# A 512-column product ahead of the 240-column one, at the double pairs that follow a block output part

## The chip, the cores and the metric

The kernel runs on one core of a Trainium2 chip. The metric is the device time of one execution in microseconds, as the median of repeated executions of the same program. The profile shows one of them, engine by engine: PE (TensorE, its weight loads listed apart as PEld), DVE (VectorE), ACT (ScalarE), POOL (GpSimd) and SP (SyncE, which issues most loads).

## The reference

One decoder block on 512 tokens of width 1024, in float32: a feed-forward network, a token mixer, a second feed-forward network, each behind a norm and with a gated residual. The change lies in the two networks. Each multiplies 1024 to 2 x 2816 columns, combines the halves, and multiplies 2816 back to 1024:

```
def swiglu(u, w_in, w_out):
    a, b = jnp.split(u @ w_in, 2, axis=-1)
    return (jax.nn.silu(a) * b) @ w_out
...
    u = modulate(rmsnorm(h, g_norm_ffn1[l]), sh1, sc1)
    h = h + 0.5 * gt1 * swiglu(u, w_ffn1_in[l], w_ffn1_out[l])
    u = modulate(rmsnorm(h, g_norm_mix[l]), sh2, sc2)
    h = h + gt2 * token_mixing(u, cos, sin, w_in[l], w_pool[l], pool_scale[l],
                               w_pool_branch[l], w_attn_branch[l], w_out[l])
    u = modulate(rmsnorm(h, g_norm_ffn2[l]), sh3, sc3)
    h = h + 0.5 * gt3 * swiglu(u, w_ffn2_in[l], w_ffn2_out[l])
return rmsnorm(h, g_final)
```

## The kernel before

Everything is kept transposed: features on the 128 partitions, the 512 tokens along the row. A float32 operand is split into a high and a low part (whi and wlo for weights, UH and UL for the network's input, HI and HK for the hidden values), and each product of the algorithm is three matmuls on PE: high x high, high x low, low x high. Weights come by DMA into the buffers raw and X, ACT writes the high part into the ring whi, and DVE (or ACT and a summing DMA of POOL) writes the low part into wlo.

The 22 hidden tiles of 128 columns, each with an a and a b half, are the "pairs" of a network. `PARTS` cuts them into five parts: 0 to 3, 4 to 7, 8 to 11, 12 to 15, 16 to 21. After each part its hidden tiles are multiplied with the rows of the output matrix and added to the residual H, so that only one part's hidden values are kept. The first pairs of a network are plain: 512-column matmuls. From the 7th pair on in the first network, from the 5th in the second, two pairs are made together by `duo`, a "double pair": token halves of 256 columns and feature halves form 2 x 2 blocks, and seven block products stand in for eight, at the price of sums of blocks on DVE and POOL. Each block product (`product`) is 24 matmuls of 256 columns. The output parts of parts 1, 2 and 3 (`BLOCKED`) are made the same way by `out_block`: seven block products of 24 matmuls, the first begun inside the last double pair of that part. Its later products wait for hidden values that DVE has just split into HI and HK. The output parts of parts 0 and 4 are plain again: 512-column matmuls, with 256-column ones at the very end.

So PE sees, per network, a run of 512-column products (part 0), then 256-column ones to the end of part 4's double pairs, then 512 again. Parts 2 and 3 are two double pairs and a block output part, 3 x 168 = 504 matmuls of 256 columns; part 4 is three double pairs, 504 too.

Two things in the code take account of where such runs meet. `room` shifts the weights in the ring by `SHIFT` = 16 columns for all chunks that are used with 256-column products. And `settle` issues one matmul of 240 columns whose result is overwritten: it writes into the bank that the next real product starts anew. `product` does this when its argument `extra` is set, which `ffn` does for the first double pair of each part.

Within a network, instructions are first recorded and then put in order: `Recorder.flush` walks a plan with a cost for each instruction, keeps PE's order as written, and picks on DVE, ACT, POOL and SP at each moment the instruction that is latest. The code's own order on PE therefore stands, and the other engines' order follows from the plan. All that is recorded has line 318 in the profile.

Of the kernel before, what the change touches and what calls it, by code (L numbers as in the profile page):

```python
# [136 lines left out]
BLOCKED = (1, 2, 3)  # L137
# [7 lines left out]
def pairs_before(n, part):  # L145

    k1 = PARTS[part][1]
    return k1 + 2 if n == 0 and part == 0 else k1
# [17 lines left out]
class Recorder:  # L166
# [24 lines left out]
    def add(self, eng, method, a, k):  # L191
        aps = lambda xs: [x for x in xs if hasattr(x, "tensor") and hasattr(x, "ap")]
        outs = aps(a[:1]) + aps([k.get("accum_out")])
        ins = aps(a[1:]) + aps(v for n, v in k.items() if n != "accum_out")
        i, deps = len(self.ops), set()
        ru = [u for x in ins for u in self.units(x)]
        wu = [u for x in outs for u in self.units(x)]
        for u in ru:
            if u in self.written:
                deps.add(self.written[u])  # L200
        for u in wu:
            if u in self.written:
                deps.add(self.written[u])
            deps.update(self.read.get(u, ()))
        for u in ru:
            self.read.setdefault(u, set()).add(i)
        for u in wu:
            self.written[u] = i
            self.read[u] = set()
        f = None  # L210
        if eng == "ACT" and method == "activation":
            f = self.SETS.get(a[2], a[2])
        elif method == "preload_act_table":
            f = a[0]
        if f is not None:
            now, at, users = self.table
            if f != now:
                deps.update(users)
                if at is not None:
                    deps.add(at)  # L220
                self.table = [f, i, []]
            else:
                deps.add(at)
                users.append(i)
        deps.discard(i)
        self.ops.append((eng, method, a, k, deps, outs, ins))
        return None
# [94 lines left out]
class Kernel:  # L322
# [6 lines left out]
    def plan(self):  # L329
# [52 lines left out]
        def ffn(n, ins, outs, first):  # L382
# [4 lines left out]
            for part, (k0, k1) in enumerate(PARTS):  # L387
# [11 lines left out]
                if part not in BLOCKED:  # L399
                    if n and part + 1 < len(PARTS):  # L400
                        self.added.update(range(len(self.order), len(self.order) + KT // 2))
                    plain(recs)

        ffn(0, f1i, f1o, FIRST)
        shift(4)
        base = len(self.order)
# [5 lines left out]
        self.shifted.update(range(base, base + 4))  # L412
        shift(3)
        ffn(2, f2i, f2o, 0)
        shift(5)
        self.fetched = self.done = self.made = 0
# [584 lines left out]
    def product(self, bank, u, start, extra=0, before=lambda: None):  # L1001
        M = self.nc.tensor.matmul
        before()
        w = self.take()
        if extra:
            self.settle(bank, w[0][0], self.UH[0])
        for p in range(2):
            o = bank[:, p * HT:(p + 1) * HT]
            for k in range(4):
                (hi, lo), (uh, ul) = w[4 * p + k], u[k]  # L1010
                M(o, hi, uh, start=start and p == 0 and k == 0, stop=False, skip_group_check=True)  # L1011
                M(o, hi, ul, start=False, stop=False, skip_group_check=True)  # L1012
                M(o, lo, uh, start=False, stop=k == 3, skip_group_check=True)  # L1013
# [202 lines left out]
    def ffn(self, n, j, last=None):  # L1216
# [10 lines left out]
            self.begin()  # L1227
        for part, (k0, k1) in enumerate(PARTS):
            tail = part + 1 == len(PARTS)
            extra = 1  # L1230
            while j < pairs_before(n, part):
                if j < PLAIN[n]:
                    self.ffn_pair(j, beside)
                    j += 1
                else:
                    own = part in BLOCKED and j + 2 == k1
                    if own and n == 0:
                        last = self.beside_out(part) or last
                    self.duo(n, j, last, tail and j + 2 == FT, extra, self.todo if own else None)
                    last, extra = None, 0  # L1240
                    j += 2
            if part in BLOCKED:
                continue
            if n == 0:
                if part == 0:
                    self.end()
                    last = self.beside_out(part)
                    self.begin()
                else:
                    last = self.beside_out(part) or last  # L1250
            if tail and n:
                self.end()
            nc, v = self.nc, self.nc.vector
            nk = k1 - k0
            hk = [self.plain_of(k) for k in range(k0, k1)]
            if not tail:
                for m in range(0, KT, 2):
                    self.look(4)
                    w = self.take()
                    bs = [self.nb(), self.nb()]  # L1260

                    for ka, kb in ((0, nk - 1), (nk - 1, nk)) if m == 0 else ():
                        for i in range(2):
                            for k in range(ka, kb):
                                self.mm3(bs[i], *w[nk * i + k], *hk[k], k == 0, k == nk - 1)
                    for i, b in enumerate(bs):
                        for k in range(nk if m else 0):
                            self.mm3(b, *w[nk * i + k], *hk[k], k == 0, k == nk - 1)
                        v.scalar_tensor_tensor(self.H[m + i], b, gate[:, m + i:m + i + 1], self.H[m + i],
                                               op0=OP.mult, op1=OP.add)  # L1270

                        if self.todo:
                            self.todo.pop(0)()
                    self.step()
                continue

            def ks(m):
                w = self.take()
                self.split_hi()
                return [(hi, lo, *hk[k]) for k, (hi, lo) in enumerate(w)]  # L1280

            self.look()
            if n == 2:
                self.sums.close()
                op = self.f2.enter_context(self.tc.tile_pool(name="f2o", bufs=1))
                self.OO = op.tile([P, KT * T], F32, name="out").rearrange("p (m t) -> p m t", m=KT)
                self.O = [self.OO[:, m, :] for m in range(KT)]

            kl = [ks(0), ks(1)]
            bs = [self.nb(), self.nb()]  # L1290
            for ka, kb in ((0, nk - 2), (nk - 2, nk)):
                for m in range(2):
                    for k in range(ka, kb):
                        self.mm3(bs[m], *kl[m][k], k == 0, k == nk - 1)
            for m in range(3 if n else 4):
                if m > 1:
                    bs.append(self.nb())
                    for k, x in enumerate(ks(m)):
                        self.mm3(bs[m], *x, k == 0, k == nk - 1)
                v.scalar_tensor_tensor(self.H[m], bs[m], gate[:, m:m + 1], self.H[m], op0=OP.mult, op1=OP.add)  # L1300
                add = self.sumsq(m, self.H[m])
                if n == 2:
                    nc.scalar.activation(self.O[m], self.H[m], AF.Copy, scale=self.g(3)[:, m:m + 1])
                self.split_lo()
                add()
                if m:
                    self.split(self.done)
                self.fetch()
            if n:
                self.out_end((3, 4, 5, 6, 7), ks, gate)  # L1310
            else:
                self.out_tail((4, 5, 6, 7), ks, gate, 1, lambda m: self.X[0][:, m % 2 * HT:])
                self.end()
# [851 lines left out]
```

## Time and profile before

| | |
|---|---|
| median of 3 runs | 1001.5 us (999.51 to 1003.51) |
| the profiled execution's own time | 999.64 us |
| its span, first to last instruction | 997.9 us |
| mean granted TensorE clock | 0.997 |
| PE busy | 980.0 us, 7120 matmuls |
| DVE busy | 798.1 us |
| ACT busy | 550.9 us |
| first 240-column product behind 512-column ones in a double pair | 102.90 us, second network 716.83 us |
| 240-column products at parts 2, 3, 4, first network | 149.46, 209.86, 269.40 us |
| 240-column products at parts 2, 3, 4, second network | 776.22, 836.69, 894.90 us |

Times in the profile count from the first instruction. A matmul is listed from its start to its modelled end, some 0.28 us for 256 columns, and the next begins long before that end; the pace of PE is therefore the distance between starts, or the count of matmuls in a stretch, and not the listed duration. A stretch's count includes those that began shortly before it.

### The profile page before, as it was taken

How to read it: one execution, taken by the hardware profiler on the slowest of the kernel's cores; microseconds unless marked ns; L12 is line 12 of the kernel's file. 1: busy time of each engine (PE TensorE's matmuls, PEld its weight loads, DVE VectorE, ACT ScalarE, POOL GpSimd, SP SyncE). 2: the span in 40 equal slices, each digit the busy share in tenths (PEclk: the TensorE clock that was granted, in tenths of full speed). 3: DMA queues.
4: the chain of work that ended last, by engine and by line, in shares of the span. 5: the costliest groups of instructions: out<-in, count | busy, mean ns of one | idle time of the engine just before them, and what ended most of it. 6: DMA issues, size and time to landing. Idle time of an engine off the chain costs nothing.

```text
span 997.9 us, 17750 instructions
## 1 busy us (share of the span) xinstructions
PE 980.0 (98%) x7120; PEld 911.8 (91%) x7120; DVE 798.1 (80%) x1194; ACT 550.9 (55%) x827; POOL 96.3 (10%) x108
## 2 busy tenths in 40 slices
PE   9999899999999999999999999999999999999997
PEld 7888889999999899778879998998899999999997
DVE  7989899898998866898887766894677868888654
ACT  5454466747665544445645553475367575676553
POOL 0000111111100000005301000001011010110002
PEclk9999999999999999999999999999999999999999
DMA  9856997988988615665236536537568576785602
GB/s 348 275 196 223 268 246 185 237 240 213 241 211 232 195 39 164 227 202 168 63 127 168 148 97 208 183 89 198 157 170 190 148 190 179 194 202 151 183 1 86
DMA packets 55974, 180.65 MB, mean 181 GB/s; under 512 B 7505, under 2 KB 10705, under 8 KB 55890
## 3 DMA queue, kind: packets, MB, share of 16 engines
q1 hardware_dynamic: 44224, 140.18, 42.5%
q0 software_dynamic: 11088, 38.80, 20.7%
q8 instruction: 56, 0.92, 0.4%
q10 hardware_dynamic: 578, 0.53, 0.2%
q14 instruction: 28, 0.23, 0.1%
HBM read 135.29 MB, written 2.24 MB: 138 GB/s over the span
## 4 chain that ended last, share of the span: by engine, by line
PE 86%; DVE 6%; issue 2%; DMA 2%; ACT 2%; SPq 1%; POOL 0%; POOLq 0%; DVEq 0%; ACTq 0%
PE bank L318 52%; PE bank L566 6%; PE bank L568 6%; PE bank L567 6%; PE bank L1011 2%; PE bank L1012 2%; PE bank L1013 2%; PE bank L2091 2%; PE bank L2093 1%; PE bank L2095 1%; DVE wlo L318 1%; DVE hf L318 1%; PE bank L1766 1%; PE bank L1468 1%; DMA X<-wf1i 1%
## 5 line engine op out<-in xcount | busy, mean ns | idle before, releaser
L318 PE MATMUL bank<-UH,whi 128*128 128x256 f32 (+2 forms) x680 | 195.8, 290 | 0.0
L318 PE MATMUL bank<-UL,whi 128*128 128x256 f32 (+1 forms) x672 | 194.9, 290 | 0.1
L318 PE MATMUL bank<-UH,wlo 128*128 128x256 f32 (+1 forms) x672 | 194.7, 290 | 0.0
L318 ACT ACTIVATE whi<-X 128x1024 fp32r<-128x1024 f32 (+3 forms) x121 | 117.1, 982 | 53.5 <-DVE X L318 26.7
L318 PE MATMUL bank<-HK,whi 128*128 128x256 f32 (+1 forms) x472 | 142.4, 302 | 3.5 <-DVE HK L318 2.2
L318 DVE TENSOR_TENSOR wlo<-X,whi 128x1024 fp32r<-128x1024 f32 (+3 forms) x111 | 124.3, 1132 | 23.5 <-ACT whi L318 23.3
L318 PE MATMUL bank<-HI,wlo 128*128 128x256 f32 (+1 forms) x472 | 141.0, 299 | 1.3 <-DVE H L318 1.2
L318 PE MATMUL bank<-HI,whi 128*128 128x256 f32 (+2 forms) x473 | 141.1, 299 | 0.0
L318 PEld LDWEIGHTS bank<-UH,whi 128*128 128x128 f32 x680 | 128.8, 190 | 2.6
L318 PEld LDWEIGHTS bank<-UL,whi 128*128 128x128 f32 x672 | 126.2, 188 | 2.8 <-DVE UL L702 0.3
L318 PEld LDWEIGHTS bank<-UH,wlo 128*128 128x128 f32 x672 | 126.2, 188 | 2.5
L318 PE MATMUL bank<-SH,whi 128*128 128x256 f32 x408 | 114.9, 282 | 3.4 <-ACT bank L318 3.4
L318 PE MATMUL bank<-SL,whi 128*128 128x256 f32 x408 | 114.6, 281 | 0.0
L318 PE MATMUL bank<-SH,wlo 128*128 128x256 f32 x408 | 114.6, 281 | 0.0
L318 PEld LDWEIGHTS bank<-HK,whi 128*128 128x128 f32 x472 | 88.8, 188 | 9.5 <-DVE HK L318 4.4
L318 ACT ACTIVATE whi<-raw 128x1024 fp32r<-128x1024 f32 (+3 forms) x94 | 80.8, 880 | 28.1 <-PE bank L318 15.4
L318 PEld LDWEIGHTS bank<-HI,wlo 128*128 128x128 f32 x472 | 88.6, 188 | 5.3 <-DVE H L318 1.4
L318 PEld LDWEIGHTS bank<-HI,whi 128*128 128x128 f32 x473 | 89.0, 188 | 3.6
L536 DVE TENSOR_TENSOR wlo<-raw,whi 128x1024 fp32r<-128x1024 f32 (+5 forms) x68 | 74.9, 1114 | 16.8 <-ACT whi L519 16.8
L318 DVE TENSOR_TENSOR wlo<-raw,whi 128x1024 fp32r<-128x1024 f32 (+3 forms) x79 | 77.0, 994 | 8.0 <-ACT whi L318 8.0
L318 PEld LDWEIGHTS bank<-SH,whi 128*128 128x128 f32 x408 | 78.5, 192 | 3.5 <-ACT bank L318 3.5
L318 PEld LDWEIGHTS bank<-SL,whi 128*128 128x128 f32 x408 | 77.3, 189 | 0.0
(388 smaller groups left out, 2256.2 us busy)
## 6 DMA issues: line engine op xcount, KB each, us to landing
raw<-wmix SPq DMA_DIRECT2D x44, 512.0 KB, 3.9
raw<-wf1i SPq DMA_DIRECT2D x31, 512.0 KB, 5.5
raw<-wf2i SPq DMA_DIRECT2D x29, 512.0 KB, 4.4
ada<-wada SPq DMA_DIRECT2D x23, 512.0 KB, 5.4
X<-X POOLq DMA_DIRECT2D x23, 512.0 KB, 4.8
AR<-wada SPq DMA_DIRECT2D x19, 512.0 KB, 5.0
raw<-raw POOLq DMA_DIRECT2D x16, 512.0 KB, 5.5
X<-wf2i SPq DMA_DIRECT2D x15, 512.0 KB, 4.6
```

The lines of the kernel that those rows point to most:

```text
L318: getattr(self.real[eng], method)(*a, **k)
L536: self.nc.vector.tensor_tensor(self.lo[:, y], r[:, x], self.hi[:, y], op=OP.subtract)
L566: M(ps, hi, uh, start=start, stop=False)
L567: M(ps, hi, ul, start=False, stop=False)
L568: M(ps, lo, uh, start=False, stop=stop)
L1011: M(o, hi, uh, start=start and p == 0 and k == 0, stop=False, skip_group_check=True)
L1012: M(o, hi, ul, start=False, stop=False, skip_group_check=True)
L1013: M(o, lo, uh, start=False, stop=k == 3, skip_group_check=True)
L1468: nc.tensor.matmul(S[:, o], q[:, toks], k[:, ks], start=True, stop=True, skip_group_check=True)
L1766: M(b, uh, hi, start=k == 0, stop=False)
L2091: M(b, hi, self.UH[k], start=k == 0, stop=False)
L2093: M(b, hi, self.UL[k], start=False, stop=False)
```

## The change

`ffn` now sets `extra` to 2 instead of 1 for the first double pair of a part whose predecessor has a block output part: parts 2, 3 and 4 of both networks, six places. `product` then issues one more matmul ahead of the 240-column one, with the same weights and the same bank, over all 512 columns of UH. Its result is overwritten as well.

```
@@ product
         w = self.take()
+        if extra > 1:
+            M(bank, w[0][0], self.UH[0], start=True, stop=True, skip_group_check=True)
         if extra:
             self.settle(bank, w[0][0], self.UH[0])
@@ ffn
-            extra = 1
+            extra = 1 + int(part - 1 in BLOCKED)
```

On PE, at the start of part 2 of the first network (149.46 us): the last products of the block output part (into bank 95), then the double pair's first block product (bank 93). Before:

```order
L318 MATMUL bank_95<-HK,whi 128x256
L318 MATMUL bank_95<-HI,wlo 128x256
L318 MATMUL bank_93<-UH,whi 128x240
L318 MATMUL bank_93<-UH,whi 128x256
L318 MATMUL bank_93<-UL,whi 128x256
```

and after:

```order
L318 MATMUL bank_95<-HK,whi 128x256
L318 MATMUL bank_95<-HI,wlo 128x256
L318 MATMUL bank_93<-UH,whi 128x512
L318 MATMUL bank_93<-UH,whi 128x240
L318 MATMUL bank_93<-UH,whi 128x256
L318 MATMUL bank_93<-UL,whi 128x256
```

One row is new. Nothing else on PE changes in the whole program but the same row at the five other places.

The plan that orders the other engines counts the longer PE queue, and rows on DVE, ACT, POOL and SP change places from part 2 of the first network on and in the second network. On DVE, at the end of the second double pair of part 2 in the second network (the rows of the trace from 818 us; hf are the hidden values before they are split, X and raw weight buffers). Before:

```order
L318 TENSOR_TENSOR HK<-hf,HI 128x256
L318 TENSOR_TENSOR HK<-hf,HI 128x1024
L318 TENSOR_TENSOR X<-raw_63,raw_65 128x1024
L318 TENSOR_TENSOR wlo<-raw_65,whi 128x512 x2
L318 TENSOR_TENSOR wlo<-raw_64,whi 128x1024
L318 SCALAR_TENSOR_TENSOR H<-bank_95,mod,H 128x256 x2
```

and after:

```order
L318 TENSOR_TENSOR HK<-hf,HI 128x256
L318 TENSOR_TENSOR wlo<-raw_65,whi 128x512
L318 TENSOR_TENSOR HK<-hf,HI 128x1024
L318 TENSOR_TENSOR wlo<-raw_65,whi 128x512
L318 TENSOR_TENSOR wlo<-raw_64,whi 128x1024
L318 SCALAR_TENSOR_TENSOR H<-bank_95,mod,H 128x256
```

A low half of weights has moved ahead of the 1024-wide HK, and the sum of two weight blocks stands earlier, outside the excerpt. The instructions are the same.

More of the change, by code (lines that the diff above doesn't have):

```diff
@@ L1004, in product @@
         w = self.take()
+        if extra > 1:
+            M(bank, w[0][0], self.UH[0], start=True, stop=True, skip_group_check=True)
         if extra:
@@ L1229, in ffn @@
             tail = part + 1 == len(PARTS)
-            extra = 1
+            extra = 1 + int(part - 1 in BLOCKED)
             while j < pairs_before(n, part):
```

## The prediction

> **What bounds the kernel now.** I read the head of the page first, for the bound; then a table of stretches, each cut from one 240-column product to the next; then the order of time on PE around those products; then the waits of PE.
>
> ```profile
> span 997.9 us, 17750 instructions
> PE 980.0 (98%) x7120; PEld 911.8 (91%) x7120; DVE 798.1 (80%) x1194; ACT 550.9 (55%) x827; POOL 96.3 (10%) x108
> PEclk9999999999999999999999999999999999999999
> PE 86%; DVE 6%; issue 2%; DMA 2%; ACT 2%; SPq 1%; POOL 0%; POOLq 0%; DVEq 0%; ACTq 0%
> ```
>
> PE is busy for 98% of the span, the chain that ended last is PE for 86%, and the granted clock stays at nine tenths or more. So time is saved only by issuing less on PE or by issuing the same faster. The second is possible, because equal products do not cost the same everywhere. In the next rows (stretch, its length, then busy time and number of instructions for PE, PEld, DVE, ACT, POOL) the first number behind PE's busy time is the point:
>
> ```profile
> 197.40:209.80 12.40, 12.40 (x112) 12.40 (x111) 11.83 (x19) 7.00 (x10) 0.89 (x1) 1.00 1.01 287
> 210.00:250.00 40.00, 40.00 (x342) 40.00 (x341) 35.55 (x47) 24.96 (x34) 6.06 (x7) 1.00 0.77 206
> 827.00:836.60 9.60, 9.60 (x84) 9.60 (x83) 7.17 (x10) 4.13 (x6) 0.86 (x1) 1.00 0.77 237
> 838.00:876.00 38.00, 38.00 (x337) 38.00 (x337) 32.16 (x41) 24.03 (x33) 4.81 (x6) 1.00 0.74 186
> 718.00:758.00 40.00, 40.00 (x356) 40.00 (x355) 28.25 (x35) 26.45 (x37) 6.06 (x7) 1.00 0.73 176
> 533.00:548.00 15.00, 15.00 (x135) 15.00 (x134) 11.48 (x15) 9.38 (x14) 0.85 (x1) 1.00 0.62 172
> ```
>
> All are 256-column products, PE never idles in them, and the clock is 1.00 in each. A product is listed for 0.28 us while the next begins after about 0.115, so some 2.4 of each count were already under way when the stretch began. Then 40.00 us hold 339.6 products in the second row (117.8 ns each) and 353.6 in the fifth (113.1 ns). There are two paces, which I call tight (about 113.3 ns from start to start) and wide (117.8): first, fourth, fifth and sixth row are tight, second and third wide. What changes the pace is seen in the order of time (start, duration, form; "x2" joins the 240-column product and the 256-column one behind it):
>
> ```profile
> 209.74 0.28 PE L318 MATMUL bank<-HI,wlo 128*128 128x256 f32 x1
> 209.86 0.39 PE L318 MATMUL bank<-UH,whi 128*128 128x240 f32 x2
> 836.57 0.28 PE L318 MATMUL bank<-HI,wlo 128*128 128x256 f32 x1
> 836.69 0.40 PE L318 MATMUL bank<-UH,whi 128*128 128x240 f32 x2
> 716.38 0.39 PE L318 MATMUL bank<-HK,whi 128*128 128x512 f32 x1
> 716.60 0.39 PE L318 MATMUL bank<-HI,wlo 128*128 128x512 f32 x1
> 716.83 0.39 PE L318 MATMUL bank<-UH,whi 128*128 128x240 f32 x2
> 530.20 0.39 PE L568 MATMUL bank<-YH,wlo 128*128 128x512 f32 x1
> 530.42 0.27 PE L572 MATMUL bank<-UH,whi 128*128 128x240 f32 x1
> ```
>
> The 240-column product at 209.86 stands behind 256-column products at the tight pace, and the pace after it is wide. The one at 836.69 stands behind the wide pace, and the pace after it is tight. Those at 716.83 and 530.42 stand behind a run of 512-column products, and the pace after them is tight. So behind 256-column products the 240 flips the pace; behind 512-column ones it leaves the tight one.
>
> The change touches six of these places. The table cut there (each of the seven stretches is 504 products of 256 columns and one of 240):
>
> ```profile
> 149.46:209.86 60.40, 59.55 (x508) 59.10 (x506) 55.13 (x77) 38.71 (x54) 8.66 (x10) 1.00 0.87 226
> 209.86:269.40 59.54, 59.26 (x508) 59.06 (x506) 53.60 (x74) 39.16 (x56) 8.67 (x10) 1.00 0.82 216
> 269.40:328.87 59.47, 59.47 (x508) 59.47 (x506) 52.42 (x67) 35.87 (x47) 4.35 (x5) 1.00 0.82 228
> 716.83:776.22 59.39, 58.16 (x507) 57.63 (x506) 45.81 (x58) 37.59 (x52) 7.79 (x9) 1.00 0.73 181
> 776.22:836.69 60.47, 59.85 (x508) 59.45 (x506) 46.02 (x63) 38.63 (x53) 6.96 (x8) 1.00 0.68 176
> 836.69:894.90 58.21, 58.00 (x508) 57.51 (x507) 50.64 (x68) 39.07 (x54) 8.69 (x10) 1.00 0.77 191
> 894.90:954.37 59.47, 59.47 (x508) 59.47 (x506) 42.99 (x50) 31.49 (x43) 3.47 (x4) 1.00 0.55 150
> ```
>
> The stretches from 269.40 and 894.90 (part 4 of each network) are wide from end to end: 59.47 / 505 = 117.8 ns. At 113.3 they would take 57.2. The others are two double pairs and a block output part, in which short waits of PE occur. Those from 716.83 and 836.69 begin tight, those from 149.46, 209.86 and 776.22 wide.
>
> **The change part by part.** *Added products.* Six of 512 columns, one at the head of the stretches from 149.46, 209.86, 269.40, 776.22, 836.69 and 894.90. Lower bound of one: 716.38 to 716.60 and on to 716.83, 0.225 us in a run. Upper bound, from the first ones behind 256-column products:
>
> ```profile
> 328.87 0.40 PE L318 MATMUL bank<-HI,whi 128*128 128x512 f32 x1
> 329.10 0.40 PE L318 MATMUL bank<-HK,whi 128*128 128x512 f32 x1
> 329.34 0.39 PE L318 MATMUL bank<-HI,wlo 128*128 128x512 f32 x1
> 549.58 0.40 PE L566 MATMUL bank<-PH,whi 128*128 128x512 f32 x1
> 549.82 0.40 PE L567 MATMUL bank<-PL,whi 128*128 128x512 f32 x1
> 550.05 0.39 PE L568 MATMUL bank<-PH,wlo 128*128 128x512 f32 x1
> ```
>
> 0.24. I take 0.23, the nearest case (a first one): 6 x 0.23 = 1.4 us. All of it is on the path, since PE waits for nothing there. Its operands are those of the 240 behind it, so it adds no new wait, and the bank is the one the 240 overwrites.
>
> *The pace behind them.* No row has a single 512 ahead of a 240, so this is bounded from both sides: wide, as behind 256-column products, or tight, as behind a run of 512s. I take tight. The rows above give the reason: at 328.87 the pace ahead was wide, at 549.58 tight, and the starts that follow are 0.23 and 0.24 apart in both. One 512 already wipes out which pace came before, so the flip, which needs the old pace, should be gone. Against it: the second 512 still takes 0.23 to 0.24 and not the 0.225 of a run, so one product does not reach the rhythm of a run.
>
> At the tight pace, part 4 gains 2 x (59.47 - 57.2) = 4.5 us. The three wide stretches with a block output part come to the mean of the two tight stretches, (59.39 + 58.21) / 2 = 58.80: 1.60 + 0.74 + 1.67 = 4.0. The stretch from 836.69 is tight already and gains nothing. Bounds: with 59.39 for all three the 4.0 is 2.2, with 58.21 it is 5.8.
>
> *Moved instructions.* The plan is reckoned anew with the longer PE queue, so rows on DVE, ACT, SP and POOL change places. The one that could reach PE is the DVE row of the second order excerpt, a 512-wide low half now ahead of the HK that the output part waits for:
>
> ```profile
> L318 DVE TENSOR_TENSOR wlo<-raw,whi 128x512 fp32r<-128x512 f32 x15 | 10.0, 686 | 1.4 <-ACT whi L318 1.4
> 820.92 1.23 DVE L318 TENSOR_TENSOR HK<-hf,HI 128x1024 fp32r<-128x1024 f32 x1 [0.79 <-ACT HI L318]
> PE bank L318 <- DVE HK L318: 2.2, 6, 0.7
> PE bank L318 <- DVE H L318: 2.4, 3, 1.2
> ```
>
> It takes 0.69 us and DVE idles 0.79 at that place, waiting for ACT: I cost it at nothing; if ACT were there earlier, it would delay that HK by up to 0.69. The swapped loads on SP and the swapped sums on POOL I cost at nothing, hidden by the chunks already split ahead of PE; if that cover is gone, a wait of the size above (0.7 to 1.2 us) appears. All waits of PE for DVE's HK and H are 4.6 us, so no reordering can gain more than that.
>
> *Cover at the tight pace.* The stretch from 149.46 keeps DVE busy 55.13 us; in 58.8 that is 94%, below the PE floor of 57.2. The second network's 46.02 is 78%. Next to be late is DVE in the first network's output parts.
>
> *Sum.* -4.5 - 4.0 + 1.4 = -7.1 us. The profiled execution took 999.64 (span 997.9 and 1.7 around it): 992.5. That execution is 1.9 below the median of 1001.5, so on the median's footing 994.4. With the bounds of the three stretches 992.6 to 996.2; with the runs' own spread of 2 us either way, 991 to 998.
>
> **A rule weighed.** The table has 342 and 356 equal products in 40.00 us, with no wait. The Trainium skill's page "TensorE: Matmul & The Clock Gate" (section "Back-to-back issue gap") gives N/2.4 + 2.5 ns, 215.8 for 512 columns and 109.2 for 256, and its section "Step-by-step: what each phase is for" says that loading the next weights takes no read bandwidth from the running product. By that there would be one pace, and the change would only add, an estimate of 6 x 0.216 = 1.3 us. The rows disagree with it, on the number of paces and on both figures.
>
> **The rivals.** *The wide pace stays or comes everywhere.* Since one 512 forgets the old pace, all six places behave alike, and if the 240 then lands in the wide pace, the five wide stretches stay and the one from 836.69 turns wide: from 58.21 to the mean of 60.40, 59.54 and 60.47, 60.14, +1.9. With the added 1.4: +3.3, 1004.8. For it speaks that a 240 behind 256-column products at the tight pace gave the wide one; against it, both quoted places with 512s ahead. It is decided by the first 256-column products behind 149.46 alone.
>
> *The products are dead weight.* The pace is set by what follows, not by what stands ahead, and the change does not do anything but issue: +1.4, 1002.9. This is the way of the page above. Against it: the pace changes exactly at the 240s.
>
> *Tight, but given back.* DVE in the first network falls behind, and the gains 1.60 and 0.74 turn into waits for HK: 7.1 - 2.3 = 4.8, 996.7; with another wait of 1.2 us, 997.9. For it speaks the 91% of DVE (55.13 of 60.40); against it, that the stretch from 836.69 is tight with DVE at 87% (50.64 of 58.21).
>
> **How the numbers follow.** Tight and kept 0.56; wide everywhere 0.26; dead weight 0.08; given back 0.10. I forecast 994.4, its own range 991 to 998. Leaving out no more than two in ten means taking in the dead weight and the middle of the wide case: 991 to 1005. A change of 0.5% is 5 us (996.5 or 1006.5), about what a measurement can tell from none. Faster: most of the first case, 0.49, and a little of the last, 0.01. Slower: the wide case with a wait of 1.2 us or more on top, 0.05. The rest, 0.45, is the same.
>
> **What would show it.** Right: behind each of the six 240s the count of products in 40 us is near 356 and no longer 342, the part 4 stretches take 57.4 to 57.5 us with the added product, the three others 58.4 to 59.6. Wrong: 342 behind 149.46, or also behind the sixth place; a first 512 that takes more than 0.24; new waits for DVE's HK in the first network's output parts that add more than 1 us to a stretch; or a granted clock under 1.00 in these stretches.

## The result and the profile after

The kernel after takes 998.05 us in the median of 20 runs (994.4 to 1002.77), the kernel before 1002.0 in 20 runs beside it (999.4 to 1005.55). The ratio is 0.9965, with a 95% interval of 0.9952 to 0.9977: some 3.5 us faster by the ratio (3.95 between the medians), about half of the forecast 7.1. The profiled execution of after took 995.91 us. The head of its page:

```profile
span 994.1 us, 17753 instructions
PE 975.2 (98%) x7126; PEld 906.3 (91%) x7126; DVE 797.4 (80%) x1194; ACT 550.7 (55%) x827; POOL 96.4 (10%) x108
PEclk9999999999999999999999999999999999999999
PE 81%; DVE 9%; issue 3%; DMA 3%; ACT 2%; SPq 1%; POOL 0%; POOLq 0%; DVEq 0%; ACTq 0%
```

PE has six products more and is busy 4.8 us less (980.0 before), at the same clock. DVE's share of the chain that ended last has grown from 6% to 9%. The table of stretches, cut at the added products (columns as in the prediction), and three windows within them:

```profile
149.54:210.76 61.22, 59.01 (x508) 58.18 (x507) 55.44 (x78) 38.59 (x54) 8.66 (x10) 1.00 0.88 228
210.76:270.54 59.78, 59.51 (x509) 59.27 (x507) 52.57 (x71) 39.05 (x56) 8.67 (x10) 1.00 0.82 210
270.54:328.00 57.46, 57.46 (x508) 57.42 (x507) 52.73 (x69) 35.53 (x47) 4.35 (x5) 1.00 0.80 236
775.14:834.04 58.90, 58.30 (x508) 57.80 (x507) 48.05 (x66) 38.74 (x53) 7.83 (x9) 1.00 0.73 181
834.04:892.82 58.78, 58.17 (x509) 57.67 (x508) 48.95 (x66) 38.47 (x53) 7.83 (x9) 1.00 0.76 189
892.82:950.28 57.46, 57.46 (x508) 57.42 (x507) 42.08 (x49) 31.66 (x43) 3.46 (x4) 1.00 0.59 156
157.00:187.00 30.00, 30.00 (x267) 30.00 (x266) 26.30 (x37) 18.44 (x28) 4.65 (x6) 1.00 0.80 213
212.00:252.00 40.00, 40.00 (x342) 40.00 (x342) 35.02 (x45) 25.01 (x35) 6.01 (x7) 1.00 0.79 201
276.00:316.00 40.00, 40.00 (x356) 40.00 (x355) 37.92 (x47) 24.79 (x34) 3.49 (x4) 1.00 0.81 224
```

The product counts give the pace as before: 267 in 30 us is tight (113.4 ns), 342 in 40 is wide, 356 in 40 is tight. Five of the six places are left tight; the one at 210.76 is entered wide and left wide. Stretch by stretch, with the added product in it:

| stretch of before | forecast change | measured |
|---|---|---|
| 149.46 | -1.37 | +0.82 |
| 209.86 | -0.51 | +0.24 |
| 269.40 | -2.04 | -2.01 |
| 776.22 | -1.44 | -1.57 |
| 836.69 | +0.23 | +0.57 |
| 894.90 | -2.04 | -2.01 |
| sum | -7.17 | -3.96 (span: -3.8) |

Both part 4 stretches came out to 0.03 us as forecast. Nearly the whole shortfall, 2.19 + 0.75 us, is in the first network's parts 2 and 3. The waits of PE in the first of them, then PE and DVE in order of time where the long one stands:

```profile
PE bank L318 <- DVE H L318: 1.3, 1, 1.3
PE bank L318 <- DVE HK L318: 0.7, 1, 0.7
```

```profile
198.99 0.28 PE L318 MATMUL bank<-HI,whi 128*128 128x256 f32 x1
200.53 0.38 PE L318 MATMUL bank<-HK,whi 128*128 128x256 f32 x1 [1.26 <-DVE H L318]
...
198.86 1.22 DVE L318 TENSOR_TENSOR wlo<-X,whi 128x1024 fp32r<-128x1024 f32 x1
199.99 0.48 DVE L318 SCALAR_TENSOR_TENSOR H<-bank,mod,H 128x256 f32<-128x256 f32 x1
200.39 1.22 DVE L318 SCALAR_TENSOR_TENSOR cs<-cs,cond 128x1024 f32<-128x1024 f32 x1
```

In the kernel before, PE has no wait for H in this stretch, and its only ones come to this:

```profile
PE bank L318 <- DVE HK L318: 0.9, 2, 0.7
```

In after the product at 200.53 starts 0.06 us after the first update of H ends. Two questions follow: what sets the pace behind a place, and what makes this wait.

### The profile page after: what moved, and what is told of

Same layout as the page of the kernel before. It is cut to its first block, busy times and chain, and to the rows that moved or that the text cites. A ratio compares the mean times of both kernels' runs of the same rounds, so it can differ in the third digit from the quotient of the medians.

```text
span 994.1 us, 17753 instructions
## 1 busy us (share of the span) xinstructions
PE 975.2 (98%) x7126; PEld 906.3 (91%) x7126; DVE 797.4 (80%) x1194; ACT 550.7 (55%) x827; POOL 96.4 (10%) x108
## 3 DMA queue, kind: packets, MB, share of 16 engines
HBM read 135.29 MB, written 2.24 MB: 138 GB/s over the span
## 4 chain that ended last, share of the span: by engine, by line
PE 81%; DVE 9%; issue 3%; DMA 3%; ACT 2%; SPq 1%; POOL 0%; POOLq 0%; DVEq 0%; ACTq 0%
PE bank L318 51%; PE bank L566 6%; PE bank L568 6%; PE bank L567 6%; PE bank L1013 2%; PE bank L1014 2%; PE bank L1015 2%; DVE ada L597 2%; DVE wlo L318 2%; DVE wlo L536 1%; DMA ada<-wada 1%; PE bank L1768 1%; PE bank L1470 1%; PE bank L1521 1%; PE bank L1769 1%
## 5 line engine op out<-in xcount | busy, mean ns | idle before, releaser
L318 PEld LDWEIGHTS bank<-SH,wlo 128*128 128x128 f32 x408 | 77.5, 190 | 0.0
```

Source lines behind the costliest of these rows:

```text
L318: getattr(self.real[eng], method)(*a, **k)
```

## Experiments on the pace

All times are against the kernel before, run beside each.

**Neither product.** At the six places `settle` and the 512 are left out, and the other engines keep the order of before, since the plan counts 240 columns more for each instruction in `heavy` (lines of `product`):

```
         if extra > 1:
-            M(bank, w[0][0], self.UH[0], start=True, stop=True, skip_group_check=True)
-        if extra:
+            self.nc.heavy.add(len(self.nc.ops))
+        elif extra:
             self.settle(bank, w[0][0], self.UH[0])
```

> Neither the 512- nor the 240-column product at the six places; the other engines keep the order of the kernel before. Theory K (what stands ahead only keeps or flips the pace: 240 alone flips, 512 and 240 together keep, nothing keeps): the pace after each of the six places is that ahead of it, part 4 of both networks takes about 57.1 us where tight, and the time is below the changed kernel by 6 x (0.23 + 0.11) = 2.0 us, so 996.0 against 1002.0 before (ratio 0.994). Theory R (the pair of 512 and 240 sets the tight pace, the 240 being what the tight pace needs): without it the pace behind the six places is wide, part 4 takes 59.3 us, and the time is that before less 0.7 us, 1001.3.

Measured: 994.49 us, 0.9935 (0.991 to 0.996). In a second kernel the plan is left to itself, by one line of `ffn`:

```
-            extra = 1 + int(part - 1 in BLOCKED)
+            extra = int(part - 1 not in BLOCKED)
```

> Neither product at the six places, as in the first experiment, but with the order on DVE, ACT, POOL and SP that the plan itself makes of it (the form in which one would write it). Theory K (nothing ahead keeps the pace; what else matters is the new order): if the order has no new wait of PE, as the first experiment, 0.9935 of before within 0.002; with a wait like the 1.4 us at 199 us of the changed kernel, 0.995. Theory R' (the order decides most, since the order of the changed kernel alone cost 5 us): anywhere from 0.990 to 1.000, and the difference to the first experiment shows as waits of PE for DVE in the output parts.

Measured: 994.42 us, 0.9935 (0.9914 to 0.9956), the same. The stretches of this second kernel's first network:

```profile
151.69:210.63 58.94, 57.99 (x506) 57.40 (x505) 54.95 (x77) 38.82 (x54) 8.69 (x10) 1.00 0.86 228
210.63:268.23 57.60, 57.60 (x507) 57.35 (x505) 51.50 (x70) 40.27 (x57) 9.53 (x11) 1.00 0.86 216
268.23:325.35 57.12, 57.12 (x507) 57.12 (x505) 52.20 (x68) 34.63 (x46) 3.50 (x4) 1.00 0.80 228
```

With nothing ahead, a tight pace simply goes on. Part 4 takes 57.12 us, 0.34 less than after: that is what the pair of 512 and 240 columns costs at each place (0.226 and 0.109 from start to start).

**The product alone, the order alone.** In the first, the six 512s are in the program while the plan counts them as nothing, so that DVE, ACT, POOL and SP keep the order of before. In the second, the plan counts them (`heavy` stands for 512 columns here), and they are left out:

```
 e2: +            if n == 512 and k.get("start") and k.get("stop") and k.get("skip_group_check"):
     +                return 0., 0.                     # in Recorder.cost
 e3: -            M(bank, w[0][0], self.UH[0], start=True, stop=True, skip_group_check=True)
     +            self.nc.heavy.add(len(self.nc.ops))
```

> The six 512-column products of the change, with DVE, ACT, POOL and SP in the order of the kernel before (the plan counts the added products as nothing). Theory K and theory R: at least five of the six places as in the changed kernel, part 4 about 57.2 us in both networks, time like the changed kernel, 998, or lower by up to 1.4 if the new wait of PE for H at 198.99 came from the new order. Theory P (the gain comes from the new order on the other engines): no gain, 1002.0 + 1.4 = 1003.4.

> The order on DVE, ACT, POOL and SP of the changed kernel, but without the six 512-column products; the 240-column ones stay. Theory K and theory R: the 240 flips the pace at the six places as before, part 4 takes 59.4 us in both networks behind a tight output part, time 1002 within 1.5. Theory P: the gain stays or grows by the 1.4 us of the products left out, 996.6 to 998.

Measured: the product alone 996.14 us, 0.9953 (0.9937 to 0.9969); the order alone 1005.69, 1.0055 (1.0034 to 1.0077). So the change has two parts of opposite sign. The order alone cost some 5.5 us, where no more than 1.5 either way was expected. Stretches of the product alone (four rows), then of the order alone (three):

```profile
150.93:210.19 59.26, 58.31 (x509) 57.68 (x507) 54.94 (x77) 38.80 (x54) 8.66 (x10) 1.00 0.87 227
210.19:268.84 58.65, 58.45 (x509) 58.14 (x507) 54.04 (x74) 39.24 (x56) 8.68 (x10) 1.00 0.87 225
268.84:326.34 57.50, 57.50 (x509) 57.45 (x507) 51.68 (x67) 35.56 (x47) 4.36 (x5) 1.00 0.83 232
833.12:893.08 59.96, 59.78 (x508) 59.29 (x507) 50.58 (x68) 39.00 (x54) 8.69 (x10) 1.00 0.76 186
```

```profile
150.27:212.22 61.95, 59.83 (x508) 59.18 (x506) 55.48 (x77) 38.59 (x54) 8.66 (x10) 1.00 0.87 224
212.22:271.77 59.55, 59.21 (x508) 59.01 (x507) 52.65 (x72) 39.16 (x56) 8.67 (x10) 1.00 0.84 212
839.24:899.47 60.23, 59.65 (x507) 59.26 (x506) 49.18 (x66) 38.58 (x53) 7.83 (x9) 1.00 0.74 184
```

Without the new order, the first stretch is 59.26, near the forecast 59.03; with it and no product, it has the same 1.3 us wait for H as after. The place at 833.12 was entered wide and stayed wide behind its 512, which the prediction had excluded: 59.96 us, 1.5 more than the forecast 58.44 (58.21 and 0.23).

The two parts do not add up: 4.7 us gained and 5.5 lost would leave the kernel slower, and it gained 3.5. The last row shows part of the reason. Without the 512, this place was entered tight and its 240 made it wide, 2.02 us more than before (58.21). In after the 512 stands there, and the place at 834.04 stays tight. So not all that the order costs alone is lost in after. Beside the products the new order as a whole shows no clear cost: 0.9953 with the old one and 0.9965 with the new, and the intervals overlap. What one moved row costs there has to be seen from a kernel that takes the row's effect away.

**Each program once more.** To see whether the pace at a place belongs to the program or to the execution, before and after were run again unchanged.

> The kernel before, unchanged, in one more profiled execution. Theory D (each wait of PE for DVE draws the pace anew): the same six places are entered at another mix of paces than tight, tight, tight, tight, wide, tight, each 240 flips what comes, and the span differs from 997.9 by the flipped stretches, 1.3 to 2.2 us each. Theory F (the pace at a place is fixed by the instructions): the same mix, span within 0.5 of 997.9 apart from other waits.

> The changed kernel, unchanged, in one more profiled execution. Theory D: another mix than tight, wide, tight, tight, tight, tight ahead of the six places; tight stays tight, a wide one stays wide or turns tight. The wait of 1.4 us for H at about 199 us is there again, since it comes from the order. Theory F: the second place is entered wide again and stays wide.

Measured: 1001.67 and 995.34 us (one execution each). The pace at entry to the six places was tight, tight, tight, tight, wide, tight in before's first profile and tight, wide, tight, wide, wide, tight in its second. So it is partly drawn per execution, at the waits of PE in the output parts. After showed the same mix twice, against the expectation that it would differ: behind its long wait for H (1.26 us, then 1.14) part 3 was entered wide in both.

**Widths inside part 4.** Part 4 has no waits, so here the pace at entry can be set. Two kernels have nothing at the six places and put products of various widths ahead of single block products within part 4 (the lines that issue them):

```
+        for c in LAB.get(lab, ()):
+            M(bank[:, :c], w[0][0], self.UH[0][:, HT - c:HT] if c < HT else self.UH[0][:, :c], start=True, stop=True,
+              skip_group_check=True)
```

> Nothing ahead of the first double pairs of parts 2, 3 and 4; instead, within part 4, where PE never waits, products whose results are overwritten are put ahead of block products, some 2.7 us or more apart: in the first network in this order 240; 240; 512; 512; 512 and 240; in the second 256; 240; 512 and 240; 256; six of 512 and 240. Theory K1 (a 512 flips too, so that 512 and 240 flip twice), from a tight start: wide, tight, wide, tight, tight; then tight, wide, wide, wide, tight. Theory K2 (a 512 does not flip, but makes the 240 behind it harmless): wide, tight, tight, tight, tight; then tight, wide, wide, wide, tight. Theory R (512 and 240 set tight whatever came): as K2, but tight behind the third place of the second network. Time about that before less 2 to 5 us, one look.

> Which products flip. As in the fourth experiment, products whose results are overwritten stand within part 4 ahead of block products; in the first network 384; 496; two of 512; two of 240; 128 columns; in the second three of 512; 224; 240 and 512; 512 and 256; three of 240. Theory N (every product that is not 256 columns flips once), from a tight start: wide, tight, tight, tight, wide; then wide, tight, tight, wide, tight. Theory M (only those that are no multiple of 32 columns, and 512, flip): tight, wide, wide, wide, wide; then wide, wide, wide, tight, wide. Two in a row from the wide pace may land in either, as 512 and 240 did.

Measured: 995.23 and 997.51 us (one execution each). Three windows, of the first kernel behind a lone 512 at 287.07 and behind 512 and 240 at 307.21, and of the second behind 240 and then 512 at 915.04:

```profile
288.00:304.00 16.00, 16.00 (x138) 16.00 (x137) 14.33 (x17) 11.42 (x15) 1.74 (x2) 1.00 0.78 209
308.00:324.00 16.00, 16.00 (x143) 16.00 (x142) 14.05 (x20) 11.49 (x16) 0.00 (x0) 1.00 0.82 281
```

```profile
916.00:932.00 16.00, 16.00 (x139) 16.00 (x138) 11.30 (x12) 9.18 (x12) 1.75 (x2) 1.00 0.61 157
```

All three were entered tight. 138 and 139 products in 16 us are wide, 143 are tight. From tight, the pace behind was wide after 240, 512, 496, 128, three 512s, and 240 then 512; it stayed tight after 256, two or three 240s, and after one or six 512s with a 240 behind them. From wide, one 240, one 224, one 384, one 512, two 512s, and 512 then 240 all led to tight. Rules by which each odd product flips the pace, or by which their number counts, fell with these rows. What fits: entered tight, the last step of widths counts. A 240 right behind 256s, or an end on 512, gives wide; a 240 behind a 512 or behind another 240 gives tight. This rule was made from these rows, and most widths stand on one place. Why it is so, and why there are two paces, no run here shows.

With the six places of all profiled executions and the two kernels above:

| ahead of the block product | entered tight | entered wide |
|---|---|---|
| nothing (18 places in three executions) | tight 16 | wide 2 |
| 240 | wide 16 of 16 | tight 4, wide 1 |
| 512 and 240 | tight 29 of 29 | wide 5, tight 4 |

The outcomes from wide in the last two rows go with a number. In the five places that stayed wide the 512 took 0.230 to 0.234 us from its start to the next, in the four that became tight 0.236. Of the single 240s, the one that stayed wide took 0.107 and the four others 0.114. So the wide pace seems to come in more than one state, which decides what the product ahead will do. This is read from these fourteen places after the fact; what the state is stays open.

## Experiments on the wait

**One row of DVE put back.** In before, DVE's row `cs` (a 1024-wide update) stands ahead of both updates of H, in after between them. This kernel puts it back and leaves all else as in after (lines of a loop; x, y and z are neighbours on DVE):

```
+            if ops[y][3].get("accum_out") is not None and bank(x) == bank(z) and str(bank(x)).startswith("bank") and not self.moved:
+                order.remove(y)
+                order.insert(order.index(x), y)
+                self.moved = True
```

> The kernel after with one row of VectorE put back where the kernel before has it: in the first network's part 2, the 1024-column update of cs stands ahead of both 256-column updates of H again, instead of between them; TensorE's program and all other rows are those of the kernel after. Theory (the row between the two H updates makes TensorE wait for the second H, and the wait and the wide entry behind it are what the gain lost): the wait of 1.3 to 1.4 us at about 199 us is gone, the stretch from 149.5 us goes from 61.2 to about 59.3 us, part 3 is entered and left tight at about 58.8 us instead of 59.8, and the time is that of the six products under the old order, 0.995 of before (0.9935 to 0.997), a span near 991.5 to 994. Rival (another moved row, or the product itself, makes the wait): the wait stays at 1 us or more, the first two stretches stay at 61.2 and 59.8, and the time is that of the kernel after, 0.9965. Second rival (the wait goes, but part 3 is entered wide anyway, by a draw at another wait): the first stretch at 59.7 and the second at 59.8, about 0.996.

Measured: 999.16 us, 0.9977 (0.996 to 0.9994). The theory fell: the wait did not go, as the rival said, and it even grew. The stretch, here also entered wide, then PE's row and the DVE rows ahead of it:

```profile
151.40:215.09 63.69, 60.42 (x508) 59.73 (x507) 55.63 (x78) 39.69 (x55) 9.23 (x11) 1.00 0.86 220
```

```profile
204.86 0.39 PE L326 MATMUL bank<-HK,whi 128*128 128x256 f32 x1 [2.41 <-DVE H L326]
...
203.18 1.22 DVE L326 SCALAR_TENSOR_TENSOR cs<-cs,cond 128x1024 f32<-128x1024 f32 x1
204.32 0.08 DVE L326 DVE_READ_ACCUMULATOR cs<-cs,cond 128x1 f32 x1
204.32 0.48 DVE L326 SCALAR_TENSOR_TENSOR H<-bank,mod,H 128x256 f32<-128x256 f32 x1
```

These rows of DVE are in the order of before, which has no such wait:

```profile
201.00 1.22 DVE L318 SCALAR_TENSOR_TENSOR cs<-cs,cond 128x1024 f32<-128x1024 f32 x1
202.14 0.48 DVE L318 SCALAR_TENSOR_TENSOR H<-bank,mod,H 128x256 f32<-128x256 f32 x1
```

PE waits for the *first* update of H, which now stands behind `cs`: 1.26 us became 2.41, the 1.14 us that `cs` takes from start to start. So the wait belongs to that update and not to its neighbours.

**What PE waits for.** The programs with their waits, row by row, show the difference. Each is the end of the twelve products that write bank 95 (columns 0 to 255 with the first six, 256 to 511 with the last six); before:

```
L318 MATMUL bank4_95<-HI_112,whi_66 128x256
L318 MATMUL bank4_95<-HK_113,whi_66 128x256
L318 MATMUL bank4_95<-HI_112,wlo_67 128x256
```

and after:

```
L318 MATMUL bank4_95<-HI_112,whi_66 128x256
L318 MATMUL bank4_95<-HK_113,whi_66 128x256 [waits DVE_49]
L318 MATMUL bank4_95<-HI_112,wlo_67 128x256
```

`flush` gives the instructions of all engines out as one list, in its plan's order of time. The update of H for columns 0 to 255 may start, by the recorder's table of columns, once the sixth product is done. In the new plan its turn falls between the tenth and the eleventh product, and a product given out behind it that writes the same bank gets a wait for it. `flush` does not know that wait. The traces agree: of the products from 198.99 on in after, the one at 200.53 waits for a semaphore of DVE, and in before the last of the twelve starts at 200.22, ahead of the update at 202.14. The order of rows on each engine, by which the prediction went, doesn't show the wait.

**The two products first.** Just before the list is given out, the eleventh and twelfth product are moved ahead of that update; every engine's own order stays that of after. The first kernel does this at that place alone. A second kernel does so at all five places of after with such an update (parts 1 and 2 of the first network, 1, 2 and 3 of the second). A third does it where neither product is issued, under the order of before (the first kernel of that kind, 0.9935), at the three places it finds there (the inside of a loop over the updates i):

```
+            for m, j in enumerate(rows):              # next products in the list, behind update i
+                if not ops[j][4] <= ahead:
+                    break
+                ahead.add(j)
+                if name(ops[j][5][0]) == name(ops[i][6][0]):
+                    n = m + 1                          # the last that writes the bank the update reads
+            for j in rows[:n]:
+                order.remove(j)
+            at = order.index(i)
+            order[at:at] = rows[:n]
```

> The kernel after, with two products of TensorE given out ahead of one update of H instead of behind it; the order on every engine is that of the kernel after, row by row. In the output part of the first network's part 2 the plan had given out the first of the two updates of H from bank 95 (its first 256 columns) between the tenth and the eleventh of the twelve products that write that bank (columns 256 to 511), so that the eleventh got a wait on VectorE. Given out behind the twelfth, that wait is off the eleventh product, and a wait on VectorE stands 16 products later, at the first low half of weights of the next block. Theory (the wait of 1.3 us at 199 us comes from the bank that both use, by the order of giving out, and not from VectorE's row order): the wait for H there is gone, nothing over 0.2 us takes its place, the stretch from 149.5 us goes from 61.2 to 59.2 to 59.8 us, and the median by at least 1.3 us against the kernel after: a ratio to before of 0.994 to 0.9955, a span of 990 to 993. If part 3 is then entered tight, its stretch is 58.6 to 58.8. Rival (VectorE is late there anyway, as the run with one row put back suggests): a wait of 1 us or more for VectorE appears at the product 16 places later, and the time stays at 0.9965.

Measured: 994.66 us, 0.9929 (0.9909 to 0.995). Its first two stretches, and DVE's rows, in the order of after:

```profile
149.04:208.33 59.29, 58.32 (x508) 57.69 (x507) 54.35 (x76) 38.43 (x54) 8.67 (x10) 1.00 0.86 223
208.33:266.47 58.14, 57.90 (x508) 57.60 (x507) 53.17 (x73) 39.10 (x56) 8.68 (x10) 1.00 0.87 227
```

```profile
199.48 0.47 DVE L334 SCALAR_TENSOR_TENSOR H<-bank,mod,H 128x256 f32<-128x256 f32 x1
199.87 1.21 DVE L334 SCALAR_TENSOR_TENSOR cs<-cs,cond 128x1024 f32<-128x1024 f32 x1
```

Against after the two stretches are 1.93 and 1.64 us shorter: no wait of 1.3 us, no wide stretch behind it, and part 3 entered and left tight. Together 3.6 us, as much as the ratios differ (0.9965 to 0.9929; the two intervals, 0.9952 to 0.9977 and 0.9909 to 0.995, do not overlap). The gain is above the expected range, since part 3 came out tight as well. The two profiled executions are only 2.2 us apart (995.91 and 993.70): this one lost at another place, entered and left wide, where after has 58.90:

```profile
771.55:831.91 60.36, 59.77 (x509) 59.33 (x507) 48.13 (x66) 38.72 (x53) 7.83 (x9) 1.00 0.69 176
```

> The same for all five places of the kernel after at which an update of H is given out between products that write the other half of its bank: first network's parts 1 and 2, second network's parts 1, 2 and 3. TensorE's waits for H there are 0.58, 1.26, 1.09, 0.58 and 0.58 us in the kernel after, 4.1 in all. Theory: all five go, and 4.1 us less some 0.2 to 0.6 for waits that stand next (for HK or wlo): a ratio to before of 0.9915 to 0.9935, PE's waits for H under 0.3 us in total. Rival (VectorE is the limit there and each wait is only put off): waits for wlo or HK of the same sizes a few products later, 0.995 to 0.9965.

Measured: 992.74 us, 0.9911 (0.9891 to 0.993); its interval overlaps that of the kernel with one place. PE's largest waits (the first stands ahead of the six places in every kernel, with 2.4 to 5.0 us), and the second network's parts 1 to 3:

```profile
PE bank L334 <- ACT bank L334: 3.3, 1, 3.3
PE bank L334 <- DVE HK L334: 1.7, 3, 0.8
PE bank L334 <- DVE wlo L334: 1.3, 1, 1.3
```

```profile
713.04:771.44 58.40, 58.36 (x506) 57.98 (x505) 45.32 (x58) 37.69 (x52) 7.79 (x9) 1.00 0.73 183
771.44:829.40 57.96, 57.93 (x508) 57.62 (x507) 47.85 (x65) 38.73 (x53) 7.83 (x9) 1.00 0.75 186
829.40:887.34 57.94, 57.91 (x509) 57.61 (x507) 48.72 (x66) 38.45 (x53) 7.83 (x9) 1.00 0.77 192
```

The waits for H are gone from the list. At four places that is a gain; in the first network's part 1 the wait was only put off, and came back as 1.26 us for wlo at 141 us, as the rival had it.

> Neither the 512 nor the 240 at the six places (with the plan that follows from that, as in the run before of the same kind, 0.9935), and the updates of H given out behind the products that write their bank, at the three places where the plan had put them between: TensorE's waits for H of 0.58, 1.22 and 0.58 us, 2.4 of that kernel's 3.0. Theory: 2.4 us less, a ratio to before of 0.990 to 0.992, a span of 989 to 991, the best of all. Rival (put off only): 0.9935.

Measured: 989.86 us, 0.9884 (0.9861 to 0.9907). This is the lowest of all: no product at the six places, and the updates given out behind their bank's products. The kernel built has the order of before, whose waits for H are 2.4 us in all. The expectation speaks of 3.0 in all, which is the figure of the kernel with its own plan. Part 4 of its two networks in the profiled execution:

```profile
265.47:324.83 59.36, 59.36 (x506) 59.36 (x505) 51.88 (x67) 35.70 (x47) 4.35 (x5) 1.00 0.80 223
886.46:943.58 57.12, 57.12 (x507) 57.12 (x505) 42.77 (x50) 31.50 (x43) 3.47 (x4) 1.00 0.58 156
```

The first was entered wide and, with nothing ahead, stayed so: 2.24 us that this execution lost by the draw.

## Why the prediction was half right

**Right.** The 240 behind 256-column products flips the pace (tight to wide 16 of 16, wide to tight 4 of 5), and with the 512 ahead of it a tight pace is kept: 29 of 29 places. Part 4 was forecast at 57.4 to 57.5 and took 57.46, twice. A first 512 takes 0.226 us from a tight pace and 0.23 to 0.236 from a wide one, as costed (0.23). DVE does not become the bound: with the list mended it is busy for 54.35 us of the 59.29 of part 2 (92%).

**Wrong: "I cost it at nothing".** This is the step that failed. The moved rows were judged by what DVE would be late with, at 820 us of the second network, and their cost came in the first, from how the list interleaves two engines. Its largest piece is the wait at 199 us with what follows from it, 3.6 us by the kernel that takes it away. That kernel's ratio, 0.9929 of about 1001.5 us, is 7.1 us, what the prediction's sum had without this step. To that digit it is luck: the interval allows 5.0 to 9.1, and the six stretches of its profile come to -6.04, with one entered and left wide. A second piece is the +0.57 at 836.69: 0.23 for the product, and the rest with a new wait for H of 0.58 us (at 882.74), where the only wait listed in before is 0.17 for HK.

**Wrong: "One 512 already wipes out which pace came before".** It doesn't: entered wide, 512 and 240 left 5 of 9 places wide. Hence part 3 of the first network, entered wide behind the long wait, stayed wide. This step fails under the old order too: of the 1.6 us by which the six stretches of the product alone fall short of the forecast (-5.56 for -7.17), 1.5 are at 833.12. The starts 0.23 apart behind both paces, on which that sentence rested, show the 512's own spacing and say nothing on the pace behind the 240.

**The rivals.** "Tight, but given back" was nearest, with the right place and a wait of the right size (1.26 for the assumed 1.2), but for another reason: not DVE falling behind, but a wait set by the list. The prediction's own sign of being wrong, a new wait of over 1 us in the first network's output parts, also came, for H and not for HK. "Dead weight" and "wide everywhere" fell with 57.46 in part 4. The rule of the Trainium skill's page "TensorE: Matmul & The Clock Gate", section "Back-to-back issue gap", one gap for each width, disagrees with the rows of after as with those of before: 342 and 356 equal products in 40 us at a clock of 1.00. The page gives N/2.4 + 2.5 as the gap of an isolated matmul, which the prediction did not say, and for 512 columns in a stream about 131 ns; here the 512s in a run start 225 ns apart.

**On the bank.** That the update and the products of one bank were kept apart in time is in the rows: products up to 198.99, update from 199.99, products from 200.53. The Trainium skill's page "PSUM — Partial Sum Buffer", section "PSUM bank collisions raise a hardware error", says that TensorE's writes and VectorE's reads of one bank must be kept apart even at different columns. No run here shows what happens otherwise; by that page the wait for the whole bank is needed, and one way to lose it is the one taken, to order the update behind all of the bank's products.

## What to carry to other kernels

When a plan gives out several engines' instructions as one list, compare the waits of the two programs and not only each engine's order: one update of 0.48 us placed between two products of the same bank held PE up for 0.75 us here with DVE idle, and for 1.43 where DVE came to it late. A product put in to steer PE's pace should be compared with putting in nothing: here the six 240s had made the pace wide, leaving them out (0.9935) did at least as well as repairing them with a 512 (0.9965, or 0.9953 under the old order), and the larger gain was in the waits. Where the pace is drawn at a wait, one profile per kernel misleads; count the places over several.

## What the runs showed of the hardware

Equal products of 256 columns run at 113.3 or 117.8 ns from start to start, at a granted clock of 1.00, and can keep either for a whole stretch of 504 (57.12 and 59.36 us). A change of width, or a wait of PE, can switch between them; in 18 of 18 places without either, the pace stayed. A width ahead does not set the pace by itself either: 512 and 240 kept a tight pace 29 times of 29, and behind the wide one the outcome went with the 512's own time (0.230 to 0.234 us: wide, 0.236: tight).

An update of H between two products of its bank costs more than its 0.48 us. At 882 us of after, with DVE idle, the product ahead starts at 881.88 and the next at 882.74: 0.86 in place of 0.113, so 0.75 us:

```profile
881.88 0.28 PE L318 MATMUL bank<-HK,whi 128*128 128x256 f32 x1
882.74 0.38 PE L318 MATMUL bank<-HI,wlo 128*128 128x256 f32 x1 [0.58 <-DVE H L318]
```
